# Hybrid decoder trunk on one core: side transposes issued together, and an FFN's first gated values multiplied behind the layer norm

## The chip, the cores and the metric
One core of one Trainium2 chip runs the whole program; the other cores are idle. The metric is the device time of one launch in microseconds (us). Before the change three runs took 965.94, 966.41 and 966.52 us, a median of 966.41.

## What is computed
The input x is 256 tokens of 1024 float32 values. Two layers follow each other, each made of three steps, and each step ends in a layer norm. ALPHA is 1.41.

```python
for l in range(DEPTH):                       # DEPTH = 2
    x = layer_norm(ALPHA * x + 0.5 * swiglu(x, ffn1_gate[l], ffn1_up[l], ffn1_down[l]), ln_g[l, 0], ln_b[l, 0])
    h = x @ w_in[l]                          # 1024 x 2560: u, q, f, v, g
    y_pool = multiscale_pool(u, pool_w[l], pool_scale[l])
    o = hgrn2_recurrence(q, f_raw, v, lb_all[l])
    y_hgrn = head_rms_norm(o, hgrn_norm_g[l]) * silu(g)
    x = layer_norm(ALPHA * x + concatenate([y_pool, y_hgrn]) @ w_out[l], ln_g[l, 1], ln_b[l, 1])
    x = layer_norm(ALPHA * x + 0.5 * swiglu(x, ffn2_gate[l], ffn2_up[l], ffn2_down[l]), ln_g[l, 2], ln_b[l, 2])
# swiglu(x, gate, up, down) = (silu(x @ gate) * (x @ up)) @ down, 2816 values wide
```

## The kernel before
**Tiling.** The 256 tokens are two halves (hf 0 and 1) of 128, one token per partition. An FFN's 2816 middle values are cut in 11 groups (g) of 256. In the program's names G(g, hf) multiplies a half by one group's gate and up weights and D(g, hf) multiplies the gated values by the down weights; GT(g) is a turned form of G for the groups in the middle, whose result needs no transposing.

**Products.** Every value is split in a high and a low part, and one product of two tiles is three matmuls of 512 columns (mm3, lines 96 to 98): high by high, high by low, low by high. ScalarE makes the high part and VectorE the low part (halves, lines 102 and 103): of each weight tile `wh`/`wl`, `xh`/`xl`, `dh`/`dl` from `raw`, of the transposed input `xt` (its high part on ScalarE, its low part on VectorE), of the transposed gated values `hth`/`htl`.

**Weights.** Each of 324 weight tiles (512 KB) is fetched by SyncE into one of five `raw` buffers, then cast by ScalarE and subtracted by VectorE. The next fetch into a buffer starts when VectorE's subtraction has freed it.

**Transposes on the side.** TensorE also turns tiles by a matmul with `ident`: the input of the next step, x, in two parts of four transposes each (Transposed.part, L186), the gated values hn of groups 0, 1, 9 and 10, two transposes a half (FFN.T, L409), kn and q of the mixer (flip, L575), the mixer's result y (L714) and u (L739). The pooling branch also has four small products with `pw` (mapped, L757), two matmul instructions each, that read the four pooled values tB.

**Their place in the program.** TensorE's instructions are written out in program order. A `Later` object counts products: `later(n, fn)` runs fn when n more products have been issued (mm3 ticks the clock), so the slot numbers in the code set between which products a transpose stands. The order on ScalarE and VectorE is decided ahead of the run by a scheduler from priorities; each of those engines then works through its list strictly as it stands.

**Around the change.** An FFN that isn't the first runs G(0,0), G(1,0), D(0,0), G(0,1), G(1,1), D(1,0), D(0,1), GT(2), D(1,1), and so on. FFN.gate makes `sil` on ScalarE (L343) and multiplies it into `hn` on VectorE (L344); T for that hn follows some products later. G(0,0) and G(1,0) run while the layer norm of the other half (lines 252 to 260, on VectorE) is still under way; that half's x is transposed inside G(1,0) and D(0,0). The mixer's half 0 is transposed inside the out-projection of half 1. FFN(l,0) and FFN(l,1) below are the first and second FFN of layer l.

Of the kernel before, what the change touches and what calls it, by code (L numbers as in the profile page):

```python
# [14 lines left out]
ALU = mybir.AluOpType  # L15
# [8 lines left out]
GW = 256  # L24
NG = DFF // GW
# [3 lines left out]
ALPHA = (2.0 * DEPTH) ** 0.25  # L29
# [45 lines left out]
def trunk(ctx: ExitStack, tc: tile.TileContext, t, out: bass.AP):  # L75
    nc = tc.nc
# [12 lines left out]
    later = Later()  # L89
# [148 lines left out]
    def load_gb(l, i):  # L238
# [3 lines left out]
        late_dma(b, t["ln_b"][l, i:i + 1, :].to_broadcast([P, D]))  # L242
        return g, b

    def layer_norm(hf, accs, scale, gb, slots, last=False):
        z = xp.tile([P, D], F32, name="x")
        st = sp.tile([P, 2, 6], F32, name="st")
        mv = sp.tile([P, 2], F32, name="mv")
        rs = sp.tile([P, 1], F32, name="rs")
        for c in range(2):  # L250
            cs = slice(c * 512, c * 512 + 512)
            nc.vector.scalar_tensor_tensor(z[:, cs], accs[c], scale, x[hf][:, cs], ALU.mult, ALU.add)  # L252
            nc.vector.bn_stats(st[:, c, :], z[:, cs])  # L253
        nc.vector.bn_aggr(mv, st.rearrange("p a b -> p (a b)"))
        nc.vector.tensor_scalar_add(rs, mv[:, 1:2], LN_EPS / ALPHA ** 2)
        nc.gpsimd.tensor_tensor(rs, rs, neghalf[:, 0:1], ALU.pow)
        for c in range(2):
            cs = slice(c * 512, c * 512 + 512)
            nc.vector.scalar_tensor_tensor(z[:, cs], z[:, cs], mv[:, 0:1], gb[0][:, cs], ALU.subtract, ALU.mult)  # L259
            nc.vector.scalar_tensor_tensor(z[:, cs], z[:, cs], rs, gb[1][:, cs], ALU.mult, ALU.add)  # L260
            if last:
                nc.sync.dma_start(out[hf * P:(hf + 1) * P, cs], z[:, cs])
        x[hf] = z
        pinned[0] = PINNED
        if not last:
            xT[hf] = Transposed(hf, z, slots)


    class FFN:
        def __init__(self, l, w, ln_i, first=False, last=False):  # L270
            gu, dn = t["gu"][l, w], t["dn"][l, w]
            self.first, self.last, self.mixer_next = first, last, not w
            self.slots = ((16, 18), (16, 18) if w else (13, 14))
            self.accs = [None, None]
            self.gw, self.dw, self.ht = {}, {}, {}
            self.ln = (l, ln_i)
            self.gb = None
            for g in range(NG):
                self.gw[g] = []
                for kq in range(4):  # L280
                    extra = (4 * g + kq) % (NW + NX) >= NW
                    self.gw[g].append(Weight(gu[g, kq], *(("x", NX) if extra else ("w", NW)),
                                             2 if first and g == 0 else 1))
                for n in {0: [], 1: [0, 1], 2: [], NG - 1: [NG - 2, NG - 1]}.get(g, [g - 1]):
                    self.dw[n] = [Weight(dn[2 * n + i], "d", ND) for i in range(2)]
# [53 lines left out]
        def gate(self, g, hf, ps):  # L339
            sil = scope[0].tile([P, GW], F32, name="sil", bufs=2)  # L340
            hn = scope[0].tile([P, GW], F32, name="hn", bufs=2)
            with tc.high_priority(offset=AHEAD):
                nc.scalar.activation(sil, ps[:, 0:GW], AF.Silu)  # L343
                nc.vector.tensor_tensor(hn, sil, ps[:, GW:2 * GW], ALU.mult)  # L344

            slots = {(NG - 1, 0): 2, (NG - 1, 1): 4, (1, 1): 4}
            later(slots.get((g, hf), 6), lambda: self.T(g, hf, hn))

        def start(self):
# [172 lines left out]
    def mixer(l, win, wout):  # L522
# [22 lines left out]
        def post_f(hf, ps):  # L545
            f = mp.tile([P, 512], F32, name="tA", bufs=2)
            nc.scalar.copy(f, ps)
            tmp = mp.tile([P, 512], F32, name="tB", bufs=2)
            ls = mp.tile([P, 512], F32, name="tC", bufs=2)
            log_sigmoid(ls, f, tmp)  # L550
            if l > 0:
                nc.vector.tensor_tensor(ls, ls, lm, ALU.add)
            kn[hf] = mp.tile([P, 512], F32, name="kn")
            nc.vector.tensor_tensor(f, ls, f, ALU.subtract)
            nc.scalar.activation(kn[hf], f, AF.Exp)
            if l > 0:
                nc.vector.tensor_tensor(tmp, ls, la, ALU.subtract)
                nc.vector.tensor_tensor(ls, ls, la, ALU.max)
                nc.scalar.activation(tmp, tmp, AF.Abs)
                nc.scalar.activation(tmp, tmp, AF.Exp, scale=-1.0)  # L560
                nc.scalar.activation(tmp, tmp, AF.Ln, bias=1.0)
                nc.vector.tensor_tensor(ls, ls, tmp, ALU.add)
            lh = mp.tile([P, 512], F32R, name="lh", bufs=2)
            ll = mp.tile([P, 512], F32R, name="ll", bufs=2)
            halves(lh, ll, ls)
            lf[hf] = (lh, ll)

            def go():
                kT[hf] = flip(kn[hf], "kT")
            later(13, go)  # L570

        def flip(nat, name):
            pt = psg.tile([P, NH * P], F32, name="gu").rearrange("p (k t) -> p k t", k=NH)
# [150 lines left out]
        def post_u(hf, ps):  # L724
            un = mp.tile([P, 512], F32, name="u")
            nc.scalar.copy(un, ps)
            if hf == 0:
                for w in (1,) + WINDOWS[:-1]:
                    sums[w] = mp.tile([P, 4 if w < 4 else 6 - w.bit_length(), PAD + P], F32, name=f"sum{w}")

            def pooled():
                for w in sums:
                    if hf == 0:
                        nc.gpsimd.memset(sums[w][:, :, 0:PAD], 0.0)
                    else:
                        nc.gpsimd.tensor_copy(sums[w][:, :, 0:PAD], sums[w][:, :, P:P + PAD])
                pt = psg.tile([P, 4 * P], F32, name="gu").rearrange("p (k t) -> p k t", k=4)
                for g in range(4):
                    nc.tensor.transpose(pt[:, g, :], un[:, g * P:(g + 1) * P], ident)  # L739
                now = slice(PAD, PAD + P)  # L740
                nc.scalar.copy(sums[1][:, :, now], pt)
                pl = mp.tile([P, 4, P], F32, name="tB", bufs=2)
                for g, w in enumerate(WINDOWS):

                    half = sums[w // 2][:, -(4 - g):, :]
                    dst = sums[w][:, :, now] if w in sums else pl[:, g:g + 1, :]
                    nc.vector.tensor_tensor(dst, half[:, :, now], half[:, :, PAD - w // 2:PAD + P - w // 2], ALU.add)
                    mean = dst[:, 0, :]
                    if hf == 0:
                        nc.vector.tensor_tensor(mean[:, 0:PAD], mean[:, 0:PAD], fix[:, g, :], ALU.mult)  # L750
                    nc.vector.scalar_tensor_tensor(pl[:, g, :], mean, 1.0 / w, sums[1][:, g, now], ALU.mult, ALU.subtract)
                later(9, lambda: mapped(pl))

            def mapped(pl):
                py = psg.tile([P, 4 * P], F32, name="gu").rearrange("p (k t) -> p k t", k=4)
                for g in range(4):
                    nc.tensor.matmul(py[:, g, :], pw[:, g, :], pl[:, g, :], start=True, stop=True)  # L757
                for g in range(4):
                    mh, ml = (m[:, g, :] for m in mt[hf])
                    sc = pscale[:, l, g:g + 1]  # L760
                    nc.scalar.activation(mh, py[:, g, :], AF.Copy, scale=sc)
                    nc.vector.scalar_tensor_tensor(ml, py[:, g, :], sc, mh.bitcast(F32), ALU.mult, ALU.subtract)
                ready[hf].add(0)
            later(5, pooled)
# [12 lines left out]
        for hf in range(2):  # L777
            if hf == 1:
                later.wait(lambda: all(len(r) == 2 for r in ready))
                guard.__exit__(None, None, None)  # L780
                guard = open_ffn()
            accs = [psa.tile([P, 512], F32, name="acc") for _ in range(2)]
            for n, kt in enumerate(WOUT_ORDER):
                later.wait(lambda: kt // 4 in ready[hf])
                wh, wl = wout[kt].parts
                for c in range(2):
                    cs = slice(c * 512, c * 512 + 512)
                    mm3(accs[c], mt[hf][0][:, kt, :], mt[hf][1][:, kt, :], wh[:, cs], wl[:, cs],
                        n == 0, n == KT - 1)
                wout[kt].used()  # L790
            if hf == 0:
                place.reverse()
            layer_norm(hf, accs, 1.0 / ALPHA, gb, (15, 17) if hf else (13, 15))
        return guard

    phases = []
# [81 lines left out]
```

## Time and profile before
| | |
|---|---|
| median of three runs | 966.41 us |
| the profiled execution | 968.72 us |
| its span (first to last instruction) | 967.0 us |
| mean granted TensorE clock | 0.998 |
| TensorE busy | 956.0 us, 99% |
| weight loads of TensorE | 806.9 us, 83% |
| VectorE busy | 653.5 us, 68% |
| ScalarE busy | 520.0 us, 54% |
| read from HBM | 178.76 MB, 186 GB/s over the span |

PE is TensorE's matmuls, PEld its weight loads, DVE VectorE, ACT ScalarE. A timeline row gives the start in us from the span's start, the duration, engine, line, operation, the tiles written and read, the count of merged instructions, and in brackets how long the engine sat idle before it and what ended that. Matmuls overlap: a matmul of 512 columns is shown with some 0.39 us, and the next one starts about 0.23 us after it did. What an instruction costs TensorE is read from the distance of the starts.

### The profile page before, as it was taken

The page shows a single profiled execution, that of the slowest core. Times are in us where ns is not written, and L with a number is a line of the kernel's source. Part 1 is how long each engine was busy: PE and PEld are TensorE (multiplying, and loading weights), DVE is VectorE, ACT ScalarE, POOL GpSimd, SP SyncE. Part 2 cuts the span into 40 slices and gives each one's busy share as a digit, 9 for nine tenths or more (in the row PEclk, how much of TensorE's full clock was granted, in tenths as well). Part 3 has the DMA queues.
Part 4 walks back from the last instruction along what each step waited for, and adds up shares of the span by engine and source line. Part 5 has one row for each costly group of instructions (what it writes and reads, how often), then busy time and mean ns, then how long its engine had stood idle before and what let it go on. Part 6 is the DMA issues. An engine that isn't in the chain of part 4 may idle for free. (4 is left out here: it accounts for less than half of the span.)

```text
span 967.0 us, 13131 instructions
## 1 busy us (share of the span) xinstructions
PE 956.0 (99%) x4814; PEld 806.9 (83%) x4814; DVE 653.5 (68%) x1093; ACT 520.0 (54%) x808; POOL 27.7 (3%) x50
## 2 busy tenths in 40 slices
PE   9999999999999999999999999999999999999996
PEld 7888888888887888888888888888888888888885
DVE  6875656669679775756676565647897896665625
ACT  6766554367455656454446555433965466645420
POOL 0000000010010000000000000000001000000000
PEclk9999999999999999999999999999999999999999
DMA  8977775333436867564346766543334377766301
GB/s 282 339 257 264 253 244 175 112 109 132 154 109 215 308 218 240 191 208 168 119 162 242 236 209 215 167 153 98 129 133 155 103 266 282 228 224 205 127 1 44
DMA packets 51521, 180.68 MB, mean 187 GB/s; under 512 B 6272, under 2 KB 6528, under 8 KB 51456
## 3 DMA queue, kind: packets, MB, share of 16 engines
q1 hardware_dynamic: 51264, 179.31, 55.2%
q8 instruction: 38, 0.62, 0.2%
q0 software_dynamic: 192, 0.53, 0.2%
q14 instruction: 27, 0.22, 0.1%
HBM read 178.76 MB, written 1.05 MB: 186 GB/s over the span
## 5 line engine op out<-in xcount | busy, mean ns | idle before, releaser
L102 ACT CAST wh<-raw 128x1024 fp32r<-128x1024 f32 (+1 forms) x204 | 210.1, 1034 | 110.2 <-DMA raw<-in_gu 40.7
L103 DVE TENSOR_TENSOR wl<-raw,wh 128x1024 fp32r<-128x1024 f32 (+1 forms) x204 | 241.4, 1198 | 24.8 <-ACT wh L102 12.7
L310 PE MATMUL gu<-xt,wh 128*128 128x512 f32 x768 | 180.6, 391 | 0.0
L103 DVE TENSOR_TENSOR dl<-raw,dh 128x1024 fp32r<-128x1024 f32 x88 | 106.9, 1223 | 100.2 <-ACT dh L102 99.9
L310 PEld LDWEIGHTS gu<-xt,wh 128*128 128x128 f32 x768 | 144.1, 188 | 31.5
L102 ACT CAST dh<-raw 128x1024 fp32r<-128x1024 f32 x88 | 92.0, 1050 | 108.3 <-DMA raw<-in_dn 104.0
L96 PE MATMUL acc<-dh,hth 128*128 128x512 f32 x352 | 139.9, 397 | 0.0
L98 PE MATMUL acc<-dh,htl 128*128 128x512 f32 x352 | 138.2, 393 | 0.0
L97 PE MATMUL acc<-dl,hth 128*128 128x512 f32 x352 | 137.5, 391 | 0.2 <-DVE dl L103 0.2
L96 PE MATMUL gu<-wh,xt 128*128 128x512 f32 x336 | 135.0, 402 | 0.0
L98 PE MATMUL gu<-wh,xt 128*128 128x512 f32 x336 | 131.6, 392 | 0.0
L97 PE MATMUL gu<-wl,xt 128*128 128x512 f32 x336 | 131.3, 391 | 0.0
L310 PE MATMUL gu<-xt,wl 128*128 128x256 f32 x768 | 99.6, 282 | 0.0
L310 PEld LDWEIGHTS gu<-xt,wl 128*128 128x128 f32 x768 | 96.8, 191 | 1.9
L333 DVE TENSOR_TENSOR sil<-gu,sil 128x256 f32<-128x256 f32 x64 | 27.0, 422 | 92.0 <-ACT sil L332 92.0
L98 PEld LDWEIGHTS acc<-dh,htl 128*128 128x128 f32 x352 | 66.0, 188 | 14.8
L97 PEld LDWEIGHTS acc<-dl,hth 128*128 128x128 f32 x352 | 66.2, 188 | 13.2 <-DVE dl L103 0.8
L96 PEld LDWEIGHTS acc<-dh,hth 128*128 128x128 f32 x352 | 66.2, 188 | 12.0
L98 PEld LDWEIGHTS gu<-wh,xt 128*128 128x128 f32 x336 | 63.1, 188 | 13.6
L97 PEld LDWEIGHTS gu<-wl,xt 128*128 128x128 f32 x336 | 63.2, 188 | 12.6
L96 PEld LDWEIGHTS gu<-wh,xt 128*128 128x128 f32 x336 | 63.1, 188 | 12.4
L310 PE MATMUL gu<-xt,xh 128*128 128x512 f32 x256 | 62.4, 396 | 0.0
(157 smaller groups left out, 1026.7 us busy)
## 6 DMA issues: line engine op xcount, KB each, us to landing
raw<-in_gu SPq DMA_DIRECT2D x172, 512.0 KB, 4.3
raw<-in_dn SPq DMA_DIRECT2D x88, 512.0 KB, 4.6
raw<-in_win SPq DMA_DIRECT2D x40, 512.0 KB, 4.4
raw<-in_wout SPq DMA_DIRECT2D x16, 512.0 KB, 4.3
lng<-in_ln_g SPq DMA_DIRECT2D x6, 512.0 KB, 4.5
lnb<-in_ln_b SPq DMA_DIRECT2D x6, 512.0 KB, 5.8
raw<-in_gu SPq DMA_DIRECT2D x8, 256.0 KB, 6.3
raw<-in_cumM SPq DMA_DIRECT2D x2, 512.0 KB, 5.1
```

Of the source, the lines that this page charges most:

```text
L96: nc.tensor.matmul(ps, lh, wh, start=start, stop=False)
L97: nc.tensor.matmul(ps, lh, wl, start=False, stop=False)
L98: nc.tensor.matmul(ps, ll, wh, start=False, stop=stop)
L102: first = nc.scalar.copy(dst_h, src)
L103: return first, nc.vector.tensor_tensor(dst_l, src, dst_h.bitcast(F32), ALU.subtract)
L310: nc.tensor.matmul(ps[i][part][:, 2 * S - w:], weight.parts[lo][:, c:c + P], x[:, 0:w], start=kt == 0 and not lo, stop=kt == KT - 1 and lo ...
L333: nc.vector.tensor_tensor(dst, p[:, 0:S], dst, ALU.add)
```

## The change
The two parts of a transposed input get the same slot, so that eight transposes stand in one row; the slot is that of the second part, one or two products behind the old place of the first. T(0,1) and T(1,1) of an FFN that isn't the first are joined: T(0,1) moves from 6 products behind its G to 10, T(1,1) from 4 to 2, which puts both behind the second product of D(1,0). In the first FFN T(1,0) and T(1,1) are joined in the same way. The mixer's transposes of kn move one slot up, to those of q, and half 0's `pw` matmuls one slot up, to the transposes of u. Last, in every FFN but the first, VectorE's multiplication for hn(0,0) is made to stand behind the last instruction of the layer norm.

```diff
             cs = slice(c * 512, c * 512 + 512)
             nc.vector.scalar_tensor_tensor(z[:, cs], z[:, cs], mv[:, 0:1], gb[0][:, cs], ALU.subtract, ALU.mult)
-            nc.vector.scalar_tensor_tensor(z[:, cs], z[:, cs], rs, gb[1][:, cs], ALU.mult, ALU.add)
+            normed[0] = nc.vector.scalar_tensor_tensor(z[:, cs], z[:, cs], rs, gb[1][:, cs], ALU.mult, ALU.add)
...
-            self.slots = ((16, 18), (16, 18) if w else (13, 14))
+            self.slots = ((18, 18), (18, 18) if w else (14, 14))
...
-                nc.vector.tensor_tensor(hn, sil, ps[:, GW:2 * GW], ALU.mult)
-
-            slots = {(NG - 1, 0): 2, (NG - 1, 1): 4, (1, 1): 4}
+                mul = nc.vector.tensor_tensor(hn, sil, ps[:, GW:2 * GW], ALU.mult)
+            if (g, hf) == (0, 0) and not self.first:
+
+                tc.add_manual_dep(mul.ins, normed[0].ins.name,
+                                  mybir.DependencyInfo(mybir.DependencyClass.NoSync, mybir.DependencyReason.DATA),
+                                  reason="behind the layer norm")
+
+            slots = {(NG - 1, 0): 2, (NG - 1, 1): 4}
+            slots.update({(1, 0): 5, (1, 1): 5} if self.first else {(0, 1): 10, (1, 1): 2})
             later(slots.get((g, hf), 6), lambda: self.T(g, hf, hn))
...
                 kT[hf] = flip(kn[hf], "kT")
-            later(13, go)
+            later(12, go)
...
-                later(9, lambda: mapped(pl))
+                later(9 - (hf == 0), lambda: mapped(pl))
...
-            layer_norm(hf, accs, 1.0 / ALPHA, gb, (15, 17) if hf else (13, 15))
+            layer_norm(hf, accs, 1.0 / ALPHA, gb, (17, 17) if hf else (15, 15))
```

On TensorE 20 interruptions of the products by transposes fewer are left: ten pairs of x, four of hn, four of kn with q, and two of `pw` with u now stand beside each other. The place of the `pw` matmuls in the out-projection of half 0, before:

```order
L96 MATMUL acc<-wh,mth 128x512
L97 MATMUL acc<-wl,mth 128x512
L98 MATMUL acc<-wh,mtl 128x512
L739 MATMUL gu<-ident,u 128x128 x4
L96 MATMUL acc<-wh,mth 128x512
L97 MATMUL acc<-wl,mth 128x512
L98 MATMUL acc<-wh,mtl 128x512
L757 MATMUL gu<-tB,pw 128x128 x4
```

and now (the lines have moved by eight):

```order
L96 MATMUL acc<-wh,mth 128x512
L97 MATMUL acc<-wl,mth 128x512
L98 MATMUL acc<-wh,mtl 128x512
L765 MATMUL gu<-tB,pw 128x128 x4
L747 MATMUL gu<-ident,u 128x128 x4
```

The products that read the pooled values tB stand one product earlier, and ahead of u's transposes. On VectorE, from the layer norm's statistics (mv) at the start of FFN(0,1) on, before:

```order
L254 BN_AGGR mv<-st 128x2
L103 TENSOR_TENSOR wl<-raw,wh 128x1024
L344 TENSOR_TENSOR hn<-sil,gu 128x256
L255 TENSOR_SCALAR rs<-mv 128x1
L259 SCALAR_TENSOR_TENSOR x<-x,mv,lng 128x512 x2
L260 SCALAR_TENSOR_TENSOR x<-x,rs,lnb 128x512 x2
L103 TENSOR_TENSOR dl<-raw,dh 128x1024
```

and now:

```order
L256 BN_AGGR mv<-st 128x2
L103 TENSOR_TENSOR wl<-raw,wh 128x1024
L257 TENSOR_SCALAR rs<-mv 128x1
L261 SCALAR_TENSOR_TENSOR x<-x,mv,lng 128x512 x2
L262 SCALAR_TENSOR_TENSOR x<-x,rs,lnb 128x512 x2
L346 TENSOR_TENSOR hn<-sil,gu 128x256
L103 TENSOR_TENSOR dl<-raw,dh 128x1024
```

The product hn(0,0) has gone behind the norm's last instruction. Some 13 us later on the same engine, hn(0,1) is the first L344 here and hn(1,1) the second, before:

```order
L344 TENSOR_TENSOR hn<-sil,gu 128x256
L103 TENSOR_TENSOR wl<-raw,wh 128x1024 x3
L103 TENSOR_TENSOR htl<-gu,hth 128x256
L103 TENSOR_TENSOR wl<-raw,wh 128x1024
L344 TENSOR_TENSOR hn<-sil,gu 128x256
L103 TENSOR_TENSOR dl<-raw,dh 128x1024 x2
```

and now:

```order
L346 TENSOR_TENSOR hn<-sil,gu 128x256
L103 TENSOR_TENSOR wl<-raw,wh 128x1024 x4
L103 TENSOR_TENSOR dl<-raw,dh 128x1024
L346 TENSOR_TENSOR hn<-sil,gu 128x256
L103 TENSOR_TENSOR dl<-raw,dh 128x1024
L103 TENSOR_TENSOR htl<-gu,hth 128x256 x2
```

Between the two there were four weight subtractions and one `htl`; now there are five subtractions. ScalarE's `sil` for hn(1,1) has likewise gone behind one `dh` cast more.

More of the change, by code (lines that the diff above doesn't have):

```diff
@@ L243, in load_gb @@
         return g, b
+    normed = [None]
     def layer_norm(hf, accs, scale, gb, slots, last=False):
```

## Prediction
> **What bounds it now.** I read the page's busy times first, then TensorE's waits, then TensorE's timeline around each place where a transpose moves, and last the timelines of VectorE and ScalarE at the same times.
>
> ```profile
> span 967.0 us, 13131 instructions
> PE 956.0 (99%) x4814; PEld 806.9 (83%) x4814; DVE 653.5 (68%) x1093; ACT 520.0 (54%) x808; POOL 27.7 (3%) x50
> ```
>
> TensorE sets the time: it is busy for 956.0 of 967.0 us, and its waits are few:
>
> ```profile
> PE gu L186 <- DVE x L260: 0.7, 1, 0.7
> PE gu L409 <- DVE hn L344: 0.2, 1, 0.2
> PE acc L97 <- DVE dl L103: 0.2, 1, 0.2
> ```
>
> So an edit counts only if it takes instructions' time off TensorE, ends one of these waits, or makes TensorE wait anew. VectorE and ScalarE have idle time on average, but each works through a fixed list, so a value can come late because of what is ahead of it there. The profiled execution took 968.72 us, 1.72 more than its span and 2.31 more than the median of 966.41. I make the sum on the span and carry it over.
>
> **What an interruption by transposes costs.** These rows are one visit of four transposes in FFN(0,0), and two visits that already stand together in layer 1's mixer (the number after "x" counts the transposes):
>
> ```profile
> 189.01 0.60 PE L186 MATMUL gu<-ident,x 128*128 128x128 f32 x4
> ...
> 189.68 0.39 PE L97 MATMUL acc<-dl,hth 128*128 128x512 f32 x1
> 189.91 0.40 PE L98 MATMUL acc<-dh,htl 128*128 128x512 f32 x1
> ```
>
> ```profile
> 745.72 0.60 PE L714 MATMUL gu<-ident,y 128*128 128x128 f32 x4
> 746.16 0.60 PE L739 MATMUL gu<-ident,u 128*128 128x128 f32 x4
> 746.51 0.47 PE L96 MATMUL gu<-wh,xt 128*128 128x512 f32 x1
> 746.83 0.39 PE L97 MATMUL gu<-wl,xt 128*128 128x512 f32 x1
> ```
>
> An undisturbed matmul starts 0.23 us after the one before (189.68 to 189.91). From the first transpose to the second matmul behind it are 0.67 us (189.01 to 189.68); less one normal step, four transposes cost 0.44. Eight together take 745.72 to 746.83, 1.11 us, less 0.23 is 0.88. That is twice 0.44: an interruption costs 0.11 us per transpose and nothing for being one. The hn visit quoted below at 327.04, two transposes, has the same price of 0.22 in the starts around it. Standing together therefore saves almost nothing: the 20 interruptions fewer are worth at most about 0.1 us, at 5 ns each, the rounding of these starts. **Term 1: −0.1** (0 to −0.4).
>
> A visit shows 0.60 us for four, and that would be another price: the Trainium skill, page "TensorE: Matmul & The Clock Gate", section "Part 4: PE-mode transpose", gives about 275 ns for a transpose inside a kernel, of which 173 ns are the access to SBUF. Paid anew at each visit, that would by estimate be 20 × 0.173 = 3.5 us saved; the starts 0.11 apart say that it is overlapped.
>
> **pw one product earlier.** The end of VectorE's pooling chain and TensorE beside it, layer 0 and then layer 1:
>
> ```profile
> 274.55 1.21 DVE L103 TENSOR_TENSOR wl<-raw,wh 128x1024 fp32r<-128x1024 f32 x1
> 275.69 0.28 DVE L751 SCALAR_TENSOR_TENSOR tB<-tB,sum 128x128 f32<-128x128 f32 x1
> ```
>
> ```profile
> 274.69 0.60 PE L739 MATMUL gu<-ident,u 128*128 128x128 f32 x4
> ...
> 275.82 1.05 PE L757 MATMUL gu<-tB,pw 128*128 128x128 f32 x8
> ```
>
> ```profile
> 752.07 0.60 PE L739 MATMUL gu<-ident,u 128*128 128x128 f32 x4
> ```
>
> ```profile
> 753.11 0.28 DVE L751 SCALAR_TENSOR_TENSOR tB<-tB,sum 128x128 f32<-128x128 f32 x1
> ```
>
> The last tB is ready at 275.97 (275.69 + 0.28), behind a weight subtraction of 1.21, and the order on VectorE is the same after the change. TensorE now comes to pw where u stood, at 274.69, and to the last product, the seventh of the eight instructions, 6 × 0.11 later, at 275.35. It waits 0.62. In layer 1 it comes at 752.07 + 0.66 = 752.73 and the value at 753.39: 0.66. Before, pw came after these ends or within a few instructions of them, so no wait shows. **Term 2: +1.3** (0.9 to 1.5: less if VectorE's chain starts a little earlier, more by the wake-up after a wait).
>
> **x in one visit of eight, mixer to second FFN.** The eight stand where the second four stood, and a product later the first G reads them. Layer 0:
>
> ```profile
> 294.78 1.05 ACT L102 CAST wh<-raw 128x1024 fp32r<-128x1024 f32 x1
> 295.90 0.58 ACT L102 CAST xt<-gu 128x512 fp32r<-128x512 f32 x1
> ```
>
> ```profile
> 295.52 0.68 DVE L252 SCALAR_TENSOR_TENSOR x<-acc,x 128x512 f32<-128x512 f32 x1
> 296.12 1.22 DVE L103 TENSOR_TENSOR wl<-raw,wh 128x1024 fp32r<-128x1024 f32 x1
> 297.25 0.68 DVE L103 TENSOR_TENSOR xt<-gu,xt 128x512 fp32r<-128x512 f32 x1
> ```
>
> ```profile
> 296.87 0.39 PE L98 MATMUL gu<-wh,xt 128*128 128x512 f32 x1
> ```
>
> Until now the first part's xt was made while the second was still to be transposed. With both at about 295, ScalarE makes xh of the first part behind a weight cast, and VectorE its low part behind x<-acc and a subtraction of 1.22. I work it out from these durations as ready near 297.5, against the matmul at 296.87 that reads it: a wait of 0.65. In layer 0 it is not added, since it falls ahead of a stretch that waits anyway (next term). In layer 1 nothing waits in the same place now, so **term 3: +0.65** (0 to 0.9). FFN(0,1) to FFN(1,0) has the same edit with the readers one product further off: **term 4: +0.3** (0 to 0.65). In the first FFN, and from FFN to mixer, I find the value at least half a microsecond ahead of its reader: nothing. kn is 2 us ahead of its new place: nothing.
>
> **hn(0,0) behind the norm.** Around the largest wait of the trace:
>
> ```profile
> 305.13 0.42 DVE L344 TENSOR_TENSOR hn<-sil,gu 128x256 f32<-128x256 f32 x1 [1.94 <-ACT sil L343]
> ```
>
> ```profile
> 307.75 0.63 PE L186 MATMUL gu<-ident,x 128*128 128x128 f32 x4 [0.73 <-DVE x L260]
> ...
> 309.80 0.50 PE L98 MATMUL acc<-dh,htl 128*128 128x512 f32 x1
> ```
>
> ```profile
> 307.37 1.05 ACT L102 CAST dh<-raw 128x1024 fp32r<-128x1024 f32 x1 [1.29 <-DMA raw<-in_dn]
> 308.32 0.37 ACT L102 CAST hth<-gu 128x256 fp32r<-128x256 f32 x1
> ```
>
> VectorE stands 1.94 us for `sil` while the layer norm is queued behind. With hn behind the norm, the norm ends about 2.3 us earlier (1.94 and most of hn's own 0.42), and the 0.73 of x goes. What is late next is D(0,0): its third matmul, L98 at 309.80, needs htl, made on VectorE from hth, and hth is cast on ScalarE until 308.69, behind a dh cast that waits for its DMA. hn itself comes about 0.8 us later than now but still ahead of that cast. So htl is there at about 309.3 whatever x does, and the matmul at 309.80 moves up by about 0.5, of which the delay of term 3 in layer 0 takes half. **Term 5: −0.25** (−1.1 to +0.3). In the other two FFNs nothing waits here now.
>
> **T(0,1) and T(1,1) two products into D(1,0).** This is the main term. hn(1,1) was transposed four products behind its G, now two: 1.37 us less (six matmuls of 0.23). T(0,1), 0.22, has also gone from ahead of it. FFN(1,0):
>
> ```profile
> 510.34 1.05 ACT L102 CAST dh<-raw 128x1024 fp32r<-128x1024 f32 x1
> 511.29 0.37 ACT L343 ACTIVATE sil<-gu 128x256 f32<-128x256 f32 x1
> ```
>
> ```profile
> 511.63 1.22 DVE L103 TENSOR_TENSOR dl<-raw,dh 128x1024 fp32r<-128x1024 f32 x1
> 512.76 0.41 DVE L344 TENSOR_TENSOR hn<-sil,gu 128x256 f32<-128x256 f32 x1
> ```
>
> ```profile
> 512.63 0.39 PE L98 MATMUL acc<-dh,htl 128*128 128x512 f32 x1
> 513.23 0.44 PE L409 MATMUL gu<-ident,hn 128*128 128x128 f32 x2 [0.21 <-DVE hn L344]
> ```
>
> TensorE is 0.37 us late there already (513.23 against 512.63 + 0.23). Its new arrival is 512.86 − 0.22 − 1.37 = 511.27. hn(1,1) does not move up as far, because `sil` still stands behind a dh cast and hn behind a subtraction: with ScalarE 0.3 us earlier I get its end between 512.4 and 513.2, taking 512.85. The wait is 1.6 instead of 0.37: **term 6a: +1.2** (0.9 to 1.7). FFN(0,1) and FFN(1,1):
>
> ```profile
> 326.16 0.41 DVE L344 TENSOR_TENSOR hn<-sil,gu 128x256 f32<-128x256 f32 x1
> ```
>
> ```profile
> 327.04 0.38 PE L409 MATMUL gu<-ident,hn 128*128 128x128 f32 x2
> ```
>
> ```profile
> 802.60 0.41 DVE L344 TENSOR_TENSOR hn<-sil,gu 128x256 f32<-128x256 f32 x1
> ```
>
> ```profile
> 802.53 0.39 PE L98 MATMUL acc<-dh,htl 128*128 128x512 f32 x1
> 803.07 0.44 PE L409 MATMUL gu<-ident,hn 128*128 128x128 f32 x2
> ```
>
> In FFN(0,1) the arrival goes from 327.04 to 325.2 (0.22, 1.37 and the 0.25 of term 5). hn(1,1) ends at 326.57 now; in the new order one weight subtraction more stands ahead of it, against an earlier start of VectorE, which gives an end of 325.6 to 326.7, mid 326.15. **Term 6b: +1.0** (0.4 to 1.5). In FFN(1,1) hn ends at 803.01 and TensorE is some 0.3 late with it (803.07 against 802.53 + 0.23 = 802.76); the new arrival is 802.76 − 1.59 = 801.17, and with the 0.65 of term 3 801.8; hn by the same bounds ends 802.6 to 803.7, so the wait is 0.8 to 1.9, less the old 0.3: **term 6c: +1.1** (0.5 to 1.6).
>
> **The sum.** −0.1 + 1.3 + 0.65 + 0.3 − 0.25 + 1.2 + 1.0 + 1.1 = +5.2 us. The profiled execution would go from 968.72 to 973.9 and the median from 966.41 to 971.6. The lower ends together give +1.2, the upper ones +8.1; all at one end is not likely, so this case alone spans 969.2 to 973.8.
>
> **The rivals.** *An interruption costs something by itself.* The first matmul behind a visit shows 0.47 (746.51) where others show 0.39 or 0.40; if those 0.08 us are lost in each, 20 fewer save 1.6, and with the whole of L186's wait and what trails it gone (about 1.1) and no new wait, the sum is −2.7: 963.7. For it speaks only that row; against it that two visits together cost twice one. It decides where the values are ready at the earlier slots, which the rows at 275.69 and 512.76 deny. Chance 0.06.
>
> *The supply keeps up.* VectorE, freed of 1.94 us of standing in every such FFN, frees raw buffers sooner, the weights come sooner, and hn(1,1) is ready as the pair is reached, so that its waits are no longer than now. Then terms 6a to 6c go, and 1.3 + 0.65 + 0.3 − 0.25 − 0.1 = 1.9 is left: 968.3. For it speaks the quoted stand of 1.94; against it that ScalarE's dh cast, behind which `sil` stands, starts when its DMA lands, and that in FFN(1,0) TensorE is early even now. If xt is in time as well, this ends at no difference. Chance 0.13, of which two thirds lie within 0.2%.
>
> *The edits fall where they say but part of the waits overlap:* a wait at pw or at x moves TensorE back, and the next value is then ready. That shortens 6c, as worked in there, and perhaps 6b, within the bounds above, and doesn't change the sign.
>
> **The numbers.** A difference under 0.2%, 1.9 us, is about what a measurement of this kernel can't tell from none. The forecast has 0.81; faster 0.06; the supply's case 0.13. Same: 0.09 from the supply's case and 0.02 from the lowest end of the forecast, 0.11. Slower: 0.83. Likeliest time 971.6. The range reaches from the supply's case at 968.3 to the upper end less the unlikely coincidence, 973.9.
>
> **What would show it.** In the profile after, TensorE's waits should hold L765 waiting for tB twice with about 0.65, L417 waiting for hn three times with 0.8 to 1.9, an xt wait of about 0.65 at the start of FFN(1,1), and no L186 wait of 0.7 at x. The starts around a visit of eight should give 0.88. It is wrong if the span falls though these waits are there (then an interruption has a price of its own), or if the hn waits are missing because `sil` and hn(1,1) come over 1 us earlier against G(1,1)'s end than now.

## The result, and the profile after

The changed kernel is slower: 976.52 us median of six runs (974.58 to 978.3) against 966.55 (965.94 to 967.08), a ratio of 1.0095 with a 95% interval of 1.0085 to 1.0105, some 9.2 us (8.2 to 10.1; the two medians lie 10.0 apart). Timed a second time the ratio was 1.0081 (1.0066 to 1.0096), 7.8 us. The forecast was +5.2, with 973.9 as its upper end: the direction holds, the size does not.

The page after, first lines, and TensorE's waits (us in total, times, longest):

```profile
span 972.8 us, 13138 instructions
## 1 busy us (share of the span) xinstructions
PE 956.8 (98%) x4814; PEld 807.5 (83%) x4814; DVE 653.3 (67%) x1093; ACT 518.7 (53%) x808; POOL 26.7 (3%) x50
```

```profile
PE gu L417 <- DVE hn L346: 4.6, 3, 1.6
...
PE gu L765 <- DVE tB L759: 1.1, 2, 0.6
PE acc L96 <- ACT wh L102: 0.7, 1, 0.7
PE gu L98 <- DVE xt L103: 0.5, 2, 0.3
PE gu L96 <- ACT xt L102: 0.4, 1, 0.4
```

TensorE's work is the same, 956.8 us against 956.0. The wait at x (L186) is gone, and the waits that the prediction named stand there: hn(1,1) three times, tB twice, xt three times. What an interruption costs is as worked out; the first FFN's visit of eight:

```profile
189.62 1.03 PE L186 MATMUL gu<-ident,x 128*128 128x128 f32 x8
190.41 0.48 PE L96 MATMUL acc<-dh,hth 128*128 128x512 f32 x1
190.73 0.40 PE L97 MATMUL acc<-dl,hth 128*128 128x512 f32 x1
```

From 189.62 to 190.73 are 1.11 us, less one step of 0.23 is 0.88, twice a visit of four. Eight joined transposes save nothing over two times four.

The pooled products in layer 0 on TensorE, then their last value on VectorE:

```profile
273.81 0.83 PE L765 MATMUL gu<-tB,pw 128*128 128x128 f32 x6
275.16 0.49 PE L765 MATMUL gu<-tB,pw 128*128 128x128 f32 x2 [0.51 <-DVE tB L759]
```

```profile
273.69 1.21 DVE L103 TENSOR_TENSOR wl<-raw,wh 128x1024 fp32r<-128x1024 f32 x1
274.82 0.28 DVE L759 SCALAR_TENSOR_TENSOR tB<-tB,sum 128x128 f32<-128x128 f32 x1
```

The seventh instruction, due at 273.81 + 0.66 = 274.47, starts at 275.16: 0.69, against 0.62 forecast. Layer 1 has 0.73 by the same reading, against 0.66.

The pair in FFN(0,1), on TensorE, VectorE and ScalarE:

```profile
324.28 0.38 PE L417 MATMUL gu<-ident,hn 128*128 128x128 f32 x2
326.15 0.44 PE L417 MATMUL gu<-ident,hn 128*128 128x128 f32 x2 [1.49 <-DVE hn L346]
```

```profile
324.54 1.23 DVE L103 TENSOR_TENSOR dl<-raw,dh 128x1024 fp32r<-128x1024 f32 x1
325.68 0.41 DVE L346 TENSOR_TENSOR hn<-sil,gu 128x256 f32<-128x256 f32 x1
```

```profile
323.46 1.05 ACT L102 CAST dh<-raw 128x1024 fp32r<-128x1024 f32 x1 [0.15 <-DMA raw<-in_dn]
324.41 0.38 ACT L345 ACTIVATE sil<-gu 128x256 f32<-128x256 f32 x1
```

T(0,1) starts at 324.28, T(1,1) would follow 0.22 later and waits until 326.15: 1.65 us. hn(1,1) stands behind a dl subtraction, and its sil behind the dh cast of the same weight tile. The other two places, FFN(1,0) and FFN(1,1), have 1.77 and 1.67 by the same reading (rows at 514.71 and 807.52):

```profile
512.72 0.38 PE L417 MATMUL gu<-ident,hn 128*128 128x128 f32 x2
514.71 0.44 PE L417 MATMUL gu<-ident,hn 128*128 128x128 f32 x2 [1.61 <-DVE hn L346]
```

```profile
805.63 0.38 PE L417 MATMUL gu<-ident,hn 128*128 128x128 f32 x2
807.52 0.44 PE L417 MATMUL gu<-ident,hn 128*128 128x128 f32 x2 [1.51 <-DVE hn L346]
```

And xt, in the first product of FFN(0,1) and in that of FFN(1,0):

```profile
296.62 0.40 PE L97 MATMUL gu<-wl,xt 128*128 128x512 f32 x1
297.24 0.50 PE L98 MATMUL gu<-wh,xt 128*128 128x512 f32 x1 [0.22 <-DVE xt L103]
297.57 0.39 PE L96 MATMUL gu<-wh,xt 128*128 128x512 f32 x1
```

```profile
484.20 0.40 PE L98 MATMUL acc<-dh,htl 128*128 128x512 f32 x1
484.96 0.50 PE L96 MATMUL gu<-wh,xt 128*128 128x512 f32 x1 [0.37 <-ACT xt L102]
485.30 0.39 PE L97 MATMUL gu<-wl,xt 128*128 128x512 f32 x1
```

The matmuls that wait come 0.39 and 0.53 us over a step of 0.23; with a smaller wait beside each it is 0.55 and 0.69, and 0.54 in FFN(1,1). The matmul right behind a late one starts 0.33 or 0.34 after it and not 0.23 (297.24 to 297.57, 484.96 to 485.30), at six places in all.

### The profile page after: what moved, and what is told of

Same layout as the page of the kernel before. It is cut to its first block, busy times and chain, and to the rows that moved or that the text cites. A ratio compares the mean times of both kernels' runs of the same rounds, so it can differ in the third digit from the quotient of the medians.

```text
span 972.8 us, 13138 instructions
## 1 busy us (share of the span) xinstructions
PE 956.8 (98%) x4814; PEld 807.5 (83%) x4814; DVE 653.3 (67%) x1093; ACT 518.7 (53%) x808; POOL 26.7 (3%) x50
```

## The experiments

Theory W is the prediction's: each edit costs the waits at its own place. S, L, Q and D are named in the expectations. Differences are against the kernel before, timed beside each run (medians 967.0 to 968.0): the ratio as a percentage with its 95% interval, then the same in us.

**Both kernels once more.**

> The kernel before, unchanged, for a second trace of it. Theory W (the new waits that the trace of the change shows are its whole price, +5.9 us): about 966.5, and a trace with the same waits as the first one, 0.9 us at x in layer 0's second FFN and 0.3 and 0.3 to 0.4 at hn(1,1). Theory S (when a weight's transfer lands decides how long TensorE waits, so that one profiled execution does not stand for the others; the first trace of before was a slow one at 968.72): 966.5, and a trace with some 2 us fewer waits than the first.

Ratio 1.0002 (0.9992 to 1.0011), and a trace of 964.3 us where the first was 967.0. TensorE at the places that the prediction quoted:

```profile
187.93 0.60 PE L186 MATMUL gu<-ident,x 128*128 128x128 f32 x4
...
305.82 0.60 PE L186 MATMUL gu<-ident,x 128*128 128x128 f32 x4
```

At the first place it is 1.08 us ahead of the first trace (187.93 against 189.01), all of it from the first 12 us of the launch; at x 1.93 (305.82 against 307.75), since the wait of 0.73 and what trails it are missing: VectorE did not stand for sil(0,0) here.

```profile
302.23 0.42 DVE L344 TENSOR_TENSOR hn<-sil,gu 128x256 f32<-128x256 f32 x1
302.57 0.15 DVE L255 TENSOR_SCALAR rs<-mv 128x1 f32<-128x1 f32 x1
```

The dh cast ahead of sil(0,0) on ScalarE waited 1.92 us for its transfer in the first trace and 0.90 here:

```profile
303.77 1.05 ACT L102 CAST dh<-raw 128x1024 fp32r<-128x1024 f32 x1 [1.92 <-DMA raw<-in_dn]
```

```profile
300.87 1.05 ACT L102 CAST dh<-raw 128x1024 fp32r<-128x1024 f32 x1 [0.90 <-DMA raw<-in_dn]
```

Of the waits for hn(1,1) only one of 0.50, in FFN(0,1), and 0.14 in FFN(1,0) are left. S holds for the traces: what the change was to remove is not there in this execution. It was the lowest of its runs (966.04 to 969.58), so I compare it with the profiled execution after, which was the lowest of its runs too. Of eight traces that have hn(0,0) ahead of the norm and x in two visits (before, e1, e4, e5, e10, e11, e12, e15), two show a wait over 0.3 us at x in layer 0's second FFN: 0.90 in the first, 0.39 in e4.

> The changed kernel, unchanged, for a second trace. W: every run within 0.5 us of 974.6, with the same three waits of 1.6 to 1.8 us for hn(1,1). S: the runs are scattered over 974.5 to 978.5, and where this trace is slower than the first, the extra time lies in the waits for hn(1,1) or for x, behind a cast that waited for its transfer.

+0.81% as told above, with runs from 974.55 to 977.61; the three waits for hn(1,1) are 2.1, 2.2 and 1.5 us. The runs are as far apart as S has it and not within W's 0.5, though both profiled executions have a span of 972.8. That transfers make the runs differ is not shown, though, since no long one was traced, and there is a rival: the granted clock. Of the changed kernel's eleven runs the three at a mean clock of 0.996 took 977.34 to 977.61 and the three at 0.998 took 974.58 to 975.11; one at 0.997 took the longest, 978.3. Of 87 runs of the kernel before for which the clock is known, the seven at 0.995 or 0.996 took 968.87 to 970.71, and the 54 at 0.998 have a median of 967.16. By estimate, a clock lower by 0.002 would by itself be 1.9 us in 967. Which is cause and which effect is open. At 0.998 the two kernels are 7.5 us apart (medians 974.63 and 967.16).

**The pair.**

```diff
-            slots.update({(1, 0): 5, (1, 1): 5} if self.first else {(0, 1): 10, (1, 1): 2})
+            slots.update({(1, 0): 5, (1, 1): 5} if self.first else {(1, 1): 4})
```

> All of the change but the pair: T(0,1) and T(1,1) of the FFNs that aren't the first stand again 6 and 4 products behind their G. W: the three waits of 1.6 to 1.8 us go, less the 0.7 that before had there, so 4.4 us less than the changed kernel, 972.1. S: the scatter of the runs goes as well, and the gain is 6 us or more, 970.5 or less. If an interruption has a price of its own: three fewer joined ones cost up to 0.5.

971.78 us, +0.43% (0.31 to 0.56): the pair is worth 3.3 us in the change, less than W's 4.4, since hn(1,1) makes TensorE wait at the old place too (0.56, 0.80 and 0.42 us), and far from S's 6 or more.

```diff
-            slots = {(NG - 1, 0): 2, (NG - 1, 1): 4, (1, 1): 4}
+            slots = {(NG - 1, 0): 2, (NG - 1, 1): 4, **({(1, 1): 4} if self.first else {(0, 1): 10, (1, 1): 2})}
```

> The kernel before with this one edit: T(0,1) 10 products and T(1,1) 2 products behind their G in the FFNs that aren't the first. W: +4.4 us, 970.9, and TensorE waits three times 1.6 to 1.8 us for hn(1,1). S: +5 to +8 with runs some us apart. The rival of the prediction (the supply keeps up): within 1 us of 966.5.

970.95 us, +0.33% (0.21 to 0.46), 3.2 us, under W's 4.4 and S's 5 to 8; waits for hn(1,1) of 1.3, 1.5 and 0.9. The supply does not keep up. Which half of the pair costs: T(1,1) alone two products earlier.

```diff
-            slots = {(NG - 1, 0): 2, (NG - 1, 1): 4, (1, 1): 4}
+            slots = {(NG - 1, 0): 2, (NG - 1, 1): 4, **({(1, 1): 4} if self.first else {(1, 1): 2})}
```

> The kernel before with T(1,1) alone moved from 4 to 2 products behind its G; T(0,1) stays at 6, so nothing is joined. Theory W (the pair costs because TensorE comes to hn(1,1) 1.37 us earlier, not because T(0,1) came later to stand with it): nearly all of the +3.3 of the pair, +2.5 to +3.3. If T(0,1) coming later to its reader D(0,1) is what costs: under +1.

+0.43% (0.29 to 0.58), 4.2 us, with nothing joined:

```profile
PE gu L409 <- DVE hn L344: 3.6, 3, 1.6
```

That is over W's range of 2.5 to 3.3, but its interval takes in the 3.2 of the pair: the early T(1,1) is the cost. The pair kept together two products later:

```diff
-            slots.update({(1, 0): 5, (1, 1): 5} if self.first else {(0, 1): 10, (1, 1): 2})
+            slots.update({(1, 0): 5, (1, 1): 5} if self.first else {(0, 1): 12, (1, 1): 4})
```

> The changed kernel with the pair T(0,1), T(1,1) kept together but two products later, behind the fourth product of D(1,0), where T(1,1) stood before. W: the wait depends on where TensorE comes to hn(1,1), not on the two standing together: 1.36 us less at each of three places, so some 3.3 us under the changed kernel, +4.1 over the kernel before, the same as with the pair taken apart. If standing together costs by itself, it stays near the changed kernel, +7.4; if an interruption has a price, it is some 0.3 below the kernel with the pair apart.

976.27 us, +0.95% (0.81 to 1.09), 9.2 us, no better than the changed kernel: W's +4.1 did not come. By the number the pair costs by standing together; the trace says how. TensorE's waits:

```profile
PE acc L96 <- ACT hth L102: 2.2, 2, 1.5
PE acc L98 <- DVE htl L103: 1.7, 3, 0.6
```

The hn waits fell to 0.5 in the same view, but now T(0,1) is the late one: D(0,1) begins right behind D(1,0) and reads the hth and htl made from it. So neither of the two places tried is free for the pair: at two products hn(1,1) isn't made, at four the reader of T(0,1) is already there. Three products were not tried. Apart, each can stand where its own value and reader allow.

**pw alone.**

```diff
-                later(9, lambda: mapped(pl))
+                later(9 - (hf == 0), lambda: mapped(pl))
```

> The kernel before with this one edit: half 0's pw matmuls one product earlier, ahead of u's transposes. W (each edit costs what the waits at its place in the trace of the change show, and the edits add up): two waits of 0.7 us for the last tB, +1.4 us over the kernel before of the same call. Rival D (the delay is made good later, because TensorE then comes later to waits that are there anyway): under +0.7, with the waits of 0.7 in the trace all the same.

+0.15% (0.06 to 0.24), 1.5 us, with waits of 0.66 and 0.72: W.

**x in one visit, alone.**

```diff
-            self.slots = ((16, 18), (16, 18) if w else (13, 14))
+            self.slots = ((18, 18), (18, 18) if w else (14, 14))
...
-            layer_norm(hf, accs, 1.0 / ALPHA, gb, (15, 17) if hf else (13, 15))
+            layer_norm(hf, accs, 1.0 / ALPHA, gb, (17, 17) if hf else (15, 15))
```

> The kernel before with this one edit: the two parts of every transposed input in one visit of eight. W: the waits for xt as in the trace of the change, 0.5 us in layer 0's second FFN, 0.7 into layer 1's first FFN and 0.5 in layer 1's second, +1.7 us. D: under +0.9. If an interruption has a price of its own of 0.08 us: ten fewer take 0.8 off either.

+0.34% (0.21 to 0.46), 3.3 us, twice W's. The waits for xt are there (0.55, 0.9 and 0.56), and besides the waits for hn(1,1) are 0.24, 1.0 and 0.64, where the second trace of the kernel before has 0.50, 0.14 and none. On VectorE in FFN(1,1), the second trace of the kernel before and then this run:

```profile
799.61 0.41 DVE L344 TENSOR_TENSOR hn<-sil,gu 128x256 f32<-128x256 f32 x1
800.46 1.23 DVE L103 TENSOR_TENSOR dl<-raw,dh 128x1024 fp32r<-128x1024 f32 x1 [0.43 <-ACT dh L102]
```

```profile
804.15 1.21 DVE L103 TENSOR_TENSOR dl<-raw,dh 128x1024 fp32r<-128x1024 f32 x1
805.28 0.41 DVE L344 TENSOR_TENSOR hn<-sil,gu 128x256 f32<-128x256 f32 x1
```

Now a dl stands ahead of hn(1,1), though this edit touches neither: the scheduler has put it there, and in FFN(0,1) too. In FFN(1,0) both dl stand ahead of it in the kernel before as well, so the order doesn't explain the 1.0 there.

**The layer norm edit**, alone in the kernel before, and then the one edit taken out of the change.

```diff
...
+            if (g, hf) == (0, 0) and not self.first:
+                tc.add_manual_dep(mul.ins, normed[0].ins.name,
+                                  mybir.DependencyInfo(mybir.DependencyClass.NoSync, mybir.DependencyReason.DATA),
+                                  reason="behind the layer norm")
```

> The kernel before with this one edit: hn(0,0) behind the layer norm's last instruction on VectorE in the FFNs that aren't the first. The prediction's term 5: between -1.1 and +0.3 us. Theory L (what was over in the sum of the change, about 1 us, comes from here: VectorE and ScalarE take up the weights in another order, and hn(1,1) comes later at its old place): +0.7 to +1.5 us, with waits for hn(1,1) of 0.4 to 0.8 us each in the three FFNs.

+0.30% (0.19 to 0.41), 2.9 us, above both ranges; L's waits are there, larger than it had them. T(0,0) waits 0.35 twice for hn(0,0), which is now later, and hn(1,1) makes TensorE wait 0.90, 0.68 and 1.08:

```profile
325.00 1.22 DVE L103 TENSOR_TENSOR dl<-raw,dh 128x1024 fp32r<-128x1024 f32 x1
326.13 0.41 DVE L346 TENSOR_TENSOR hn<-sil,gu 128x256 f32<-128x256 f32 x1
```

Again that dl, and the same in FFN(1,1). In the kernel before, hn(1,1) comes first in these two and both dl behind it; in FFN(1,0) the order is as before, so the growth there to 0.68 is not explained by it. The tile is the first of D(2), which comes only after GT(2) and D(1,1).

> The changed kernel without the edit that puts hn(0,0) behind the layer norm. Theory Q (the edit makes the scheduler put one dh cast ahead of sil(1,1) and one dl subtraction ahead of hn(1,1), so hn(1,1) comes about 0.8 us later, and TensorE, which comes there early, pays it three times): 2 to 3 us under the changed kernel, +5 over the kernel before, with hn waits of 1.3 to 1.5 in place of 1.6 to 2.1. Rival D (the waits overlap, so one edit less changes little): less than 1 us under the changed kernel.

975.36 us, +0.78% (0.65 to 0.91), 7.6 us: D. The same dl stands ahead of hn(1,1) without this edit, FFN(0,1):

```profile
324.94 1.23 DVE L103 TENSOR_TENSOR dl<-raw,dh 128x1024 fp32r<-128x1024 f32 x1
326.08 0.41 DVE L346 TENSOR_TENSOR hn<-sil,gu 128x256 f32<-128x256 f32 x1
```

The x edit, which is still in, brings it as well, and the waits stay (1.9, 1.7 and 1.5). The four edits alone add up to 3.2 + 1.5 + 3.3 + 2.9 = 10.9, and the whole is 7.8 to 9.2. That fits a cost that two edits bring and that is paid once; with intervals of about 1 us each way on every term the sums alone don't show it.

**The order of that tile.** Its dh cast is held behind sil(1,1), its dl subtraction behind hn(1,1), in every FFN but the first (act and mul are those two instructions, w.halves the tile's cast and subtraction):

```diff
...
+            if (g, hf) == (1, 1) and not self.first:
+                w = self.dw[2][0]
+                if w.parts:
+                    order = mybir.DependencyInfo(mybir.DependencyClass.NoSync, mybir.DependencyReason.DATA)
+                    tc.add_manual_dep(w.halves[0].ins, act.ins.name, order, reason="behind sil")
+                    tc.add_manual_dep(w.halves[1].ins, mul.ins.name, order, reason="behind hn")
```

> The kernel before with the layer norm edit (which alone cost +2.9 us), and besides the first weight tile of D(2) held behind hn(1,1): its dh cast behind sil(1,1) on ScalarE and its dl subtraction behind hn(1,1) on VectorE. Theory Q (the layer norm edit costs because the scheduler now puts this tile ahead of hn(1,1)): the waits for hn(1,1) shrink from 0.9, 0.7 and 1.1 to 0.5 or less, and some +1 us over the kernel before is left, from hn(0,0) itself. If the order of this tile is not the cause: still +2.5 to +3.

967.85 us, +0.06% (-0.03 to 0.15): the 2.9 us are gone but for 0.6. In FFN(0,1), VectorE and TensorE:

```profile
324.89 0.41 DVE L346 TENSOR_TENSOR hn<-sil,gu 128x256 f32<-128x256 f32 x1
325.22 2.35 DVE L103 TENSOR_TENSOR dl<-raw,dh 128x1024 fp32r<-128x1024 f32 x2
```

```profile
324.94 0.39 PE L98 MATMUL acc<-dh,htl 128*128 128x512 f32 x1
325.36 0.44 PE L421 MATMUL gu<-ident,hn 128*128 128x128 f32 x2
```

The wait is 0.19 where it was 0.90, and none over 0.1 is left in the other two FFNs. Q is shown for the layer norm edit. The cast and the subtraction were held together, so which of the two counts is open, and the x edit was not run with the tile held.

> The changed kernel with the same tile held behind sil(1,1) and hn(1,1). Theory Q: each of the three waits for hn(1,1) of 1.6 to 2.1 us is 0.5 to 1.2 us shorter, so 2 to 3 us under the changed kernel, +5 to +6 over before. If the tile is not the cause: +7.5 to +9, as the changed kernel.

973.2 us, +0.62% (0.49 to 0.74), 6.0 us, as Q expected; the interval lies under that of the first timing of the changed kernel and overlaps that of the second (0.66 to 0.96). The waits for hn(1,1) shrink to 0.69 in FFN(0,1) and next to nothing in the other two; htl of T(0,1) comes late instead, with 0.5 to 0.8 in each:

```profile
PE acc L98 <- DVE htl L103: 1.4, 3, 0.6
...
PE gu L423 <- DVE hn L346: 0.5, 1, 0.5
```

> The kernel before with the same tile held behind sil(1,1) and hn(1,1); there the scheduler has it ahead of hn(1,1) only in layer 1's first FFN. Theory Q: the wait of 0.5 us for hn(1,1) in that FFN goes, 0 to 0.6 us faster than before. If the wait has another cause: no difference.

-0.04% (-0.13 to 0.05): no difference that can be told; in this trace TensorE doesn't wait for hn(1,1) at all.

**Joins at which nothing waits, and T(1,1) later.**

```diff
-            self.slots = ((16, 18), (16, 18) if w else (13, 14))
+            self.slots = ((16, 18), (16, 18) if w else (14, 14))
...
-            slots = {(NG - 1, 0): 2, (NG - 1, 1): 4, (1, 1): 4}
+            slots = {(NG - 1, 0): 2, (NG - 1, 1): 4, (1, 1): 4, **({(1, 0): 5, (1, 1): 5} if self.first else {})}
...
-            later(13, go)
+            later(12, go)
```

> The kernel before with only those transposes joined at which no wait showed: x from an FFN to the mixer in half 1, the first FFN's T(1,0) with T(1,1), kn with q: seven interruptions fewer. Theory W (an interruption costs nothing by itself): within 0.4 us of the kernel before, and the starts around a visit of eight give 0.88 us. If an interruption has a price of 0.08 us: 0.6 us less.

-0.01% (-0.09 to 0.08), that is within 0.9 us either way. This doesn't rule out 0.6 us by itself; the starts above do. The 173 ns that the Trainium skill ("TensorE: Matmul & The Clock Gate", "Part 4: PE-mode transpose") gives for the access to SBUF would by estimate save 7 × 0.173 = 1.2 us if paid at each visit. That lies outside this interval.

> The kernel before with T(1,1) of the FFNs that aren't the first two products later, 6 behind its G instead of 4; its reader D(1,1) comes only behind GT(2). Theory W (TensorE comes to hn(1,1) too early even before the change): the hn wait of 0.3 to 0.5 us that the second trace of before shows goes, and the kernel is 0.3 to 1.0 us faster than before. If the wait then stands at another place: no difference.

-0.04% (-0.13 to 0.05): none. The wait for hn is gone, and TensorE waits at GT(2) for an htl instead; layer 1's second FFN:

```profile
804.52 0.86 PE L310 MATMUL gu<-xt,xh 128*128 128x512 f32 x3
806.29 0.73 PE L310 MATMUL gu<-xt,xh 128*128 128x512 f32 x2 [0.92 <-DVE htl L103]
```

No version was faster than the kernel before.

## Why the prediction was wrong in size

**What held.** Term 1: an interruption has no price of its own (0.88 for eight), so the rival that wanted a gain was out. Term 2: pw was forecast at 1.3, shows 1.42 in the trace and costs 1.5 timed alone. The main term's mechanism: TensorE reaches hn(1,1) 1.37 us sooner and waits; early T(1,1) alone gives it all. Direction and the list of waits are as forecast.

**The step that failed most: term 5, hn(0,0) behind the norm, put at −0.25.** Alone it costs 2.9 (e7). The gain was the wait at x, which most traces lack; the cost is the order further on, where the scheduler puts a weight tile ahead of hn(1,1). The orders shown with the change have that tile, and the prediction has it as "one weight subtraction more", but books it with the pair and sets VectorE's earlier start against it. With the tile held behind hn(1,1), the norm edit costs 0.6 (e13) and the whole change 6.0 (4.7 to 7.2) in place of 7.8 to 9.2 (e14); the forecast of 5.2 lies within that. The same hold changes nothing in the kernel before (e15). The layer norm edit or the x edit brings this order, each without the pair; what it costs under the x edit alone was not tested.

**Terms 3 and 4, x: +0.65 and +0.3.** 1.78 in the trace: 0.54 in layer 1 as forecast, 0.69 instead of 0.3 into FFN(1,0), and 0.55 in layer 0, which was left out as absorbed by a stretch "that waits anyway"; in most traces it does not. The longer step behind a late matmul, six times 0.1, was not in the sum either. Timed alone the edit costs 3.3, the waits for hn(1,1) included.

**Terms 6a to 6c: +3.3.** Waits of 1.77, 1.65 and 1.67 against 1.6, 1.0 and 1.4. In FFN(0,1) hn(1,1) ended where it was put (326.09 against 326.15), but TensorE came at 324.50 and not at 325.2; the slower start of the first execution of before, 0.8 us behind this one's, is part of that. Timed alone the pair is 3.2, in the whole 3.3: the size of this term was right against the runs.

**The base, and luck.** "I make the sum on the span and carry it over" is the other weak step. The sum put the profiled execution at 973.9, and it took 974.58. That this comes so near is luck: the new waits were larger than forecast, and the first execution of before, 968.72 and above all six runs that the result was compared with (up to 967.08), held time that the change did not remove. Against the second trace of before it lost 1.1 us in the first 12 us and 1.6 at x and right behind it; the sum counted nothing of the first and 0.25 of the second. The prediction calls the 0.73 at x the largest wait of that trace; 1.1 for `zero` and 0.9 for a weight, at the start of the launch, are longer. Measured from the second trace, a span of 964.3, the change is +8.5 us: hn(1,1) 5.09 less 0.64 is 4.45, pw 1.42, xt 1.78, together 7.65; 0.3 lies in the first 12 us. The remaining 0.6 is about what the longer step behind the late xt matmuls takes; smaller differences both ways nearly cancel. The profiled execution after was the lowest of its six runs, 1.9 under their median; what the others waited for was not traced, and five of them had a lower granted clock than its 0.998.

## What to carry to other kernels

When a scheduler orders an engine's queue, look through the whole stretch behind an edit for a long instruction that has gone ahead of a short one on the path; here a subtraction of 1.2 us, which the layer norm edit does not touch, cost more than that edit did at its own place (2.9 with it, 0.6 without). Take a second profiled execution before crediting the removal of a wait that ends in a transfer: a wait that one execution shows and the next lacks is neither a gain nor a base. A transpose has a window between its value and its reader; joining two is free only where their windows overlap, and even there it saves nothing if a visit has no price of its own.

## What the runs showed of the hardware

Transposes of 128 columns start 0.11 us apart whether two, four or eight stand together (shown as 0.38, 0.60 and 1.03 us), though each is shown with some 0.27 us. Behind a matmul that had to wait the next one started 0.33 or 0.34 us later, against 0.23 in an undisturbed row. The same kernel's executions differ by up to 4 us (966.75 to 970.71 in fifteen runs of the kernel before), and the longest have the lowest granted clock (0.995 at 970.71). Two traces of it, both with a granted clock of 0.998, differ by 2.7 us. Of these 1.1 lie in the first 12 us, where the matmuls of the first trace start 0.43 us apart until 10.3 and those of the second 0.23 apart from 6.0 on, wherever none waits:

```profile
8.17 0.63 PE L96 MATMUL acc<-wh,xt 128*128 128x512 f32 x1
8.60 0.63 PE L97 MATMUL acc<-wl,xt 128*128 128x512 f32 x1
```

```profile
7.81 0.39 PE L96 MATMUL acc<-wh,xt 128*128 128x512 f32 x1
8.04 0.39 PE L97 MATMUL acc<-wl,xt 128*128 128x512 f32 x1
```

The rest lies in waits further on, most of it at x, behind casts that waited longer for their transfers.
